# The entry of a windowed attention stage: three engines in written order, the first keys' norm moved behind the first queries' norm, and more projection columns ahead of the S5 tables

## The chip, the core and the metric

The kernel runs on one core of a Trainium2 chip. The metric is the device time of one execution in microseconds (us), the median of the runs. TensorE (PE in the profile, PEld its weight loads) does the matmuls, VectorE is DVE, ScalarE is ACT, GpSimd is POOL, and SP is the engine that issues most of the DMAs. PSUM is the memory that the matmuls write; a buffer of it is called a bank here.

## What is computed

One layer of a hybrid encoder over two sequences of 512 tokens with 1024 features, all in float32. Cut to what matters here:

```python
h = rms_norm(x, ln1)
q, k, v, u, g_att, g_ssm = split(h @ w_in)
q = rms_norm(q per head, q_gain); k = rms_norm(k per head, k_gain)   # 16 query heads, 4 key heads of 64
y_att = windowed_attention(q, k, v, sink, bias, mask)                # blocks of 128, each sees 3 key blocks
y_ssm = s5_branch(u, ...)     # bidirectional state-space scan in 64 groups, GELU, gated linear unit
mixed = sigmoid(g_att) * y_att + sigmoid(g_ssm) * y_ssm
x = x + mixed @ w_out
out = x + square(relu(rms_norm(x, ln2) @ w_up)) @ w_down
```

## The kernel before

Each float32 matmul is made of three, on a high part and a low part of both operands: high times high, high times low, low times high (`products`, L190, and `key_products`, L230). ScalarE writes the high part of a weight (`S.copy`, L180 for the columns, L1086 for whole blocks), VectorE subtracts it from the raw weight for the low part (L181, L1087).

**Fillers.** The projection of `u` and of the two gates is cut into 24 columns of 128 features; a column is computed for both sequences, 24 matmuls of 512 columns for each. Behind the 24 columns come the keys of the second sequence: four tiles of 128 tokens, 24 matmuls of 256 columns each (`key_products`), each tile followed by its norm: a square on ScalarE (L239), a sum on VectorE (L241), an add and a power of minus one half on GpSimd (L243, L244), and a multiply on VectorE (L247), which is the last to read the tile's bank. All of this is one generator, and `pull(n)` takes the next matmuls from it worth n units: a matmul of a column costs 2, one of a key tile 1. The other stages call `pull` between their own steps, so that TensorE has work while they wait. `phase["units"]` is what is left. While a column is computed, the weights of the next one are split into high and low parts at its fourth and tenth matmul, and the loads behind them are issued.

**Stages, in order.** First the norms and transposes of the input, with the coefficients of the state-space branch. Then the tables: `tables(c)` for c = 0 to 7, each in two steps q. A step makes `bpre` on VectorE (L592 to L595), transposes it on TensorE (L605) into `tps`, makes the table `ctab` on VectorE (L618 to L622), and pulls 44 units. The matmuls of the inputs with `u_sb` (L636) come one step later, and the lags (L548) every second step. Then the recurrence: 62 steps on VectorE (L711 to L714), with `pull(15)` after each. Then the outputs of the state-space branch: 32 steps of 12 matmuls (L745, L748), with a share of the remaining units after each, such that about 100 are left over; these are pulled after the last step. The tables `ctab`, the inputs `u_sb` and `toep` of that loop are loaded by GpSimd's queue two to three blocks of two steps ahead.

**The attention's entry** follows. The weights of the first query heads (`w_q`) and of the values (`w_v`) are loaded (`w_in`) and split in halves of 512 KB; the last key tile's multiply is done (`last_keys.pop()()`); for t = 0 to 3 a query tile of 128 tokens is projected (L915, 24 matmuls of 256 columns), squared on ScalarE (L921), summed (L925), raised to the power (L927, L928 on GpSimd) and multiplied (L932); the query tile before it is transposed (L937) and split (L942, L945); and a value tile of the second sequence is projected (`rows_block`, L121 to L123) and split (L849, L850). For t = 0 the keys `kn[:, 0:4]` of the first sequence, which were computed at the very start, are normed: a square into `k_sq` (L1110), a sum (L1111), add and power (L1112, L1113), and, behind the first value tile, the multiply (L1124) and the copy `kd` on GpSimd (L884). The transposes of these keys (`key_turn`, L897) come in the third round.

Every projection here takes its bank from one ring of three (`acc()`), in the order in which the program calls it; the second user after the next waits for the last reader of the first. In the entry the order is: the four key tiles, query tile 0, value tile 0, query tile 1, the transposes of query tile 0, value tile 1, query tile 2, and so on.

**Who sets the order.** Inside `tc.manual_schedule(engines={...})` the engines listed run their instructions in the order in which the program writes them. The other engines are ordered by a planner with its own estimate of costs: among the instructions that it holds for ready it takes the one that the program writes first. In the tables only TensorE and GpSimd are listed; in the output loop TensorE, ScalarE and VectorE; in the attention's entry only VectorE; in the attention itself all but SP.

## Time and profile before

| | |
|---|---|
| median of 3 runs | 1470.11 us (1470.04 to 1471.46) |
| the profiled execution, its own time | 1468.74 us |
| its span in the profile | 1467.0 us |
| TensorE busy | 1441.2 us, 98% of the span |
| VectorE, ScalarE, GpSimd busy | 1099.3, 764.4, 234.2 us |
| moved by DMA | 240.23 MB, 164 GB/s in the mean |

The profile's busy times add up the instructions of an engine; a bracket behind a row of the timeline gives the idle time of the engine ahead of it and what ended that. The views by windows give for each engine its busy us and the number of its instructions, then PEclk, the share of its full clock that TensorE was granted, the share of the DMA engines' time, and the rate in GB/s.

### The profile page before, as it was taken

The numbers are of one execution on the slowest core, as the hardware profiler recorded it, in microseconds if no ns is written. First come the engines' busy times: TensorE is split into PE (matmuls) and PEld (weight loads), VectorE is DVE, ScalarE is ACT, GpSimd is POOL, SyncE is SP. The second block draws the span as 40 slices with busy tenths as digits, with TensorE's granted clock in tenths as the row PEclk, the third lists the DMA queues.
The fourth block names the chain that finished last, engine by engine and source line by source line (L and its number), as shares of the span: only waits on it lengthen the run. The fifth ranks groups of instructions, "written<-read, shape, count | busy, mean of one in ns | idle before, by whom it ended". The sixth has DMA issues, their size and how long they took to land.

```text
span 1467.0 us, 22018 instructions
## 1 busy us (share of the span) xinstructions
PE 1441.2 (98%) x7981; PEld 1228.4 (84%) x7981; DVE 1099.3 (75%) x1985; ACT 764.4 (52%) x1361; POOL 234.2 (16%) x386
## 2 busy tenths in 40 slices
PE   8899999999989999999999999999999999999998
PEld 6688888889979999987888888888888888888887
DVE  7999949995436899988985578777776588575653
ACT  7588852224336888786443345544544444333332
POOL 3144452004233433252100000000000000000000
PEclk9999999999999999999999999999999999999999
DMA  7256649428750533345553245444443883454441
GB/s 292 94 156 184 191 132 337 158 101 292 260 178 20 175 95 108 97 160 167 185 193 113 88 140 198 148 154 144 146 149 115 326 324 125 158 177 153 129 129 58
DMA packets 102204, 240.23 MB, mean 164 GB/s; under 512 B 12330, under 2 KB 25130, under 8 KB 102096
## 3 DMA queue, kind: packets, MB, share of 16 engines
q1 hardware_dynamic: 62160, 139.68, 29.5%
q0 software_dynamic: 16320, 48.28, 9.9%
q10 hardware_dynamic: 23616, 50.87, 9.3%
q8 instruction: 63, 1.03, 0.3%
q14 instruction: 45, 0.37, 0.1%
HBM read 169.02 MB, written 81.82 MB: 171 GB/s over the span
## 4 chain that ended last, share of the span: by engine, by line
PE 85%; DVE 6%; DMA 3%; ACT 2%; issue 2%; POOL 1%; SPq 0%; DVEq 0%; ACTq 0%; POOLq 0%
PE acc L190 17%; PE bank L121 13%; PE bank L122 13%; PE bank L123 13%; PE acc L915 5%; PE acc L123 2%; PE acc L121 2%; PE acc L122 2%; PE acc L128 2%; PE sps L636 2%; PE po L998 2%; PE sps L748 2%; PE sps L966 2%; PE tps L982 2%; PE acc L343 1%
## 5 line engine op out<-in xcount | busy, mean ns | idle before, releaser
L190 PE MATMUL acc<-act,c_hi 128*128 128x512 f32 x768 | 244.4, 396 | 0.0
L122 PE MATMUL bank<-b_lo,a_hi 128*128 128x512 f32 (+1 forms) x449 | 174.6, 389 | 0.1
L121 PE MATMUL bank<-b_hi,a_hi 128*128 128x512 f32 (+1 forms) x449 | 174.5, 389 | 0.0
L123 PE MATMUL bank<-b_hi,a_lo 128*128 128x512 f32 (+1 forms) x449 | 174.5, 389 | 0.0
L190 PEld LDWEIGHTS acc<-act,c_hi 128*128 128x128 f32 x768 | 142.8, 189 | 28.2 <-ACT act L316 0.9
L1649 ACT CAST a_hi<-d_a 128x1024 fp32r<-128x1024 f32 x56 | 59.0, 1054 | 177.9 <-PE bank L122 174.6
L190 PE MATMUL acc<-act,c_lo 128*128 128x512 f32 x384 | 151.4, 394 | 0.0
L121 PE MATMUL bank<-act,act 128*128 128x512 f32 x368 | 143.2, 389 | 0.3 <-DVE tx L1437 0.3
L123 PE MATMUL bank<-act,act 128*128 128x512 f32 x368 | 143.2, 389 | 0.0
L122 PE MATMUL bank<-act,act 128*128 128x512 f32 x368 | 143.2, 389 | 0.0
L1650 DVE TENSOR_TENSOR a_lo<-d_a,a_hi 128x1024 fp32r<-128x1024 f32 x56 | 68.5, 1223 | 97.0 <-ACT a_hi L1649 97.0
L915 PE MATMUL acc<-w_hi,act 128*128 128x256 f32 x512 | 115.6, 294 | 3.8 <-DVE keys L247 3.8
L122 PEld LDWEIGHTS bank<-b_lo,a_hi 128*128 128x128 f32 x449 | 84.3, 188 | 18.1 <-DVE b_lo L1650 0.5
L121 PEld LDWEIGHTS bank<-b_hi,a_hi 128*128 128x128 f32 x449 | 84.3, 188 | 17.4
L123 PEld LDWEIGHTS bank<-b_hi,a_lo 128*128 128x128 f32 x449 | 84.3, 188 | 17.3
L915 PEld LDWEIGHTS acc<-w_hi,act 128*128 128x128 f32 x512 | 88.2, 192 | 7.7 <-ACT w_hi L1086 4.0
L190 PEld LDWEIGHTS acc<-act,c_lo 128*128 128x128 f32 x384 | 72.5, 189 | 14.3
L976 ACT ACTIVATE p<-p,nmx 128x257 f32<-128x257 f32 (+1 forms) x128 | 72.1, 563 | 19.7 <-DVE nmx L970 17.6
L121 PEld LDWEIGHTS bank<-act,act 128*128 128x128 f32 x368 | 69.1, 188 | 14.8 <-issue 0.7
L128 PE MATMUL acc<-act,gc_hi 128*128 128x512 f32 x256 | 81.1, 394 | 0.2 <-ACT gc_hi L781 0.2
L123 PEld LDWEIGHTS bank<-act,act 128*128 128x128 f32 x368 | 69.1, 188 | 14.5
L122 PEld LDWEIGHTS bank<-act,act 128*128 128x128 f32 x368 | 69.1, 188 | 14.3
(356 smaller groups left out, 3424.4 us busy)
## 6 DMA issues: line engine op xcount, KB each, us to landing
d_a<-a_scr SPq DMA_DIRECT2D x56, 512.0 KB, 3.6
raws<-in_w_up_dram SPq DMA_DIRECT2D x32, 512.0 KB, 4.0
a_scr<-t ACTq DMA_DIRECT2D x64, 256.0 KB, 2.8
k<-in_w_down_dram SPq DMA_DIRECT2D x32, 512.0 KB, 5.9
c_raw<-in_w_ug_dram SPq DMA_DIRECT2D x48, 256.0 KB, 3.9
ct_scr<-ctab POOLq DMA_DIRECT2D x16, 512.0 KB, 5.4
ctab_in<-ct_scr POOLq DMA_DIRECT2D x16, 512.0 KB, 6.4
a_scr<-a ACTq DMA_DIRECT2D x32, 256.0 KB, 2.0
```

What stands on the lines that cost most here:

```text
L121: PE.matmul(ps, a[0], b[0], start=first, stop=False)
L122: PE.matmul(ps, a[0], b[1], start=False, stop=False)
L123: PE.matmul(ps, a[1], b[0], start=False, stop=last)
L128: PE.matmul(ps, w[wi][:, k, :], rows[yi], start=k + p == 0, stop=k == KT - 1 and p == 2)
L190: PE.matmul(ps, w[wi][:, k, :], hT[s][hi][:, k, :], start=n == 0, stop=n == 3 * KT - 1)
L636: PE.matmul(ps[:, i * P:(i + 1) * P], bm[:, ri, g, :], u_sb[:, gp * SH + g, :], start=True, stop=True)
L748: PE.matmul(o, ctab[:, g0 % SI + g, ri, 0:T * CH], st[:, ri, g].rearrange("p s k -> p (s k)"), start=False, stop=ri == 1)
L915: PE.matmul(self.ps, hT[sq][act][:, k, col:col + P], w[:, k % 4, :], start=i == 0, stop=i == 3 * KT - 1)
L966: PE.matmul(ps[:, 0:self.nk], qs, kk[:, self.k0 * P:self.k1 * P], start=i == 0, stop=i == 1)
L976: S.activation(p, p, AF.Exp, bias=self.nmx[:, h:h + 1], scale=-1.0, accum_out=self.sums[:, h, self.qb:self.qb + 1])
L1649: S.copy(hi, src)
L1650: V.tensor_sub(lo, src, hi.bitcast(F32))
```

## The change

Four edits. More units are pulled ahead of the tables (116 for 72). The output loop leaves 108 units over in place of 100, and its tail is no longer pulled behind it: the attention's entry pulls all but the last key tile at its head, and the last key tile behind the split of `w_q`. In the entry TensorE and ScalarE, too, run in written order. The norm of the first sequence's keys moves: square, sum and power from ahead of the first query tile's norm to behind the first value tile, the multiply and the copy from the first round to the second; and `k_sq` is a tile of the pool `ap` (tag `ya`, which the raw weights of `w_q` use) in place of the pool `evp` (tag `ev`, which the last columns use until they are stored).

```diff
             pending = []
-            pull(72)
+            pull(116)
             for c in range(KT):
                 tables(c)
...
-                pull(-(-(phase["units"] - 100) // (GROUPS // SH - q)))
+                pull(-(-(phase["units"] - 108) // (GROUPS // SH - q)))
...
             store_y(*full)
-            pull(phase["units"])
             order.close()
...
-        with tc.manual_schedule(engines={ET.DVE}):
+        with tc.manual_schedule(engines={ET.PE, ET.DVE, ET.Activation}):
+            pull(phase["units"] - 3 * KT)
             SP.dma_start(kn[:, 0:4], kv_scr[:, :, 0])
             w_q = whole_block(w_qkv[Q_BLK], wq, "ya", 2)
             weights[0] = w_q
+            pull(phase["units"])
             w_v = whole_block(w_qkv[V_BLK], cpool, "p", 3)
             last_keys.pop()()
...
-            k_sq = evp.tile([P, NB, N_KV, HD], F32, tag="ev", name="k_sq")
...
                 new.project(3 * KT)
-                if t == 0:
-                    S.activation(k_sq, kn[:, 0:4], AF.Square, scale=HD ** -0.5)
-                    V.reduce_sum(ms, k_sq.rearrange("p t h d -> p (t h) d"), axis=AX.X)
-                    GP.tensor_scalar_add(ms, ms, EPS)
-                    GP.tensor_tensor(rk, ms, neg_half, op=ALU.pow)
                 new.square()
...
                 rows_block(w_v, NB + t, v_evac)
                 if t == 0:
+                    k_sq = ap.tile([P, NB, N_KV, HD], F32, tag="ya", name="k_sq")
+                    S.activation(k_sq, kn[:, 0:4], AF.Square, scale=HD ** -0.5)
+                    V.reduce_sum(ms, k_sq.rearrange("p t h d -> p (t h) d"), axis=AX.X)
+                    GP.tensor_scalar_add(ms, ms, EPS)
+                    GP.tensor_tensor(rk, ms, neg_half, op=ALU.pow)
+                if t == 1:
                     V.tensor_mul(kn[:, 0:4], kn[:, 0:4],
                                  rk.rearrange("p (t h) -> p t h", t=NB)[:, :, :, None].to_broadcast([P, NB, N_KV, HD]))
                     kd = key_copies(0, 0)
-                if t == 1:
                     S.copy(va[:, 0:4, :, 0:HD], vn)
```

## The prediction

> **What bounds the kernel now.** I read the page's head, then TensorE's waits, then the timeline of the engines around the longest of them, then windows for the granted clock, and the chain of waits between 400 and 455 us.

> ```profile
> span 1467.0 us, 22018 instructions
> PE 1441.2 (98%) x7981; PEld 1228.4 (84%) x7981; DVE 1099.3 (75%) x1985; ACT 764.4 (52%) x1361; POOL 234.2 (16%) x386
> ...
> PE tps L605 <- issue: 4.9, 1, 4.9
> PE acc L915 <- DVE keys L247: 3.8, 1, 3.8
> PE acc L937 <- DVE qn L932: 3.0, 2, 2.9
> ```

> TensorE is busy all but 26 us. Less work on another engine gives nothing; what counts is a hole in TensorE's row and the slow stretch behind it. Three long waits lie where the diff works: one ahead of the tables, two in the attention's entry. The hole ahead of the tables:

> ```profile
> 60.74 0.39 PE L190 MATMUL acc<-act,c_lo 128*128 128x512 f32 x1
> 66.00 2.10 PE L605 MATMUL tps<-ident,bpre 128*128 128x128 f32 x8 [4.88 <-issue]
> 73.98 1.95 PE L636 MATMUL sps<-u_sb,bm 128*128 128x128 f32 x16
> 75.77 1.04 PE L605 MATMUL tps<-ident,bpre 128*128 128x128 f32 x8
> ...
> 65.22 1.28 DVE L595 TENSOR_TENSOR bpre<-tb,bpre 128x512 f32<-128x512 f32 x2
> 70.44 0.69 DVE L181 TENSOR_TENSOR c_lo<-c_raw,c_hi 128x512 fp32r<-128x512 f32 x1
> 72.84 1.29 DVE L595 TENSOR_TENSOR bpre<-tb,bpre 128x512 f32<-128x512 f32 x2
> ...
> 66.25 0.62 ACT L180 CAST c_hi<-c_raw 128x512 fp32r<-128x512 f32 x1 [3.30 <-DMA c_raw<-in_w_ug_dram]
> ```

> The 72 units end at 61.12; the first transposes need `bpre`, which VectorE finishes only around 66. The profile calls the releaser "issue", but the engine that ends last is VectorE. The two holes in the entry:

> ```profile
> 409.33 0.38 ACT L239 ACTIVATE keys<-acc 128x256 f32<-128x256 f32 x1 [1.87 <-PE acc L230]
> 416.13 1.06 ACT L1110 ACTIVATE k_sq<-kn 128x1024 f32<-128x1024 f32 x1 [6.41 <-DMA gs_scr<-sg]
> 418.12 0.38 ACT L239 ACTIVATE keys<-acc 128x256 f32<-128x256 f32 x1
> 421.20 0.42 DVE L247 TENSOR_TENSOR keys<-acc,rk 128x256 f32<-128x256 f32 x1 [1.25 <-POOL rk L244]
> 417.65 0.28 PE L230 MATMUL acc<-c_hi,act 128*128 128x256 f32 x1
> 421.77 0.55 PE L915 MATMUL acc<-w_hi,act 128*128 128x256 f32 x1 [3.84 <-DVE keys L247]
> ...
> 428.45 1.21 DVE L1111 TENSOR_REDUCE k_ms<-k_sq 128x16 f32<-128x1024 f32 x1
> 429.27 0.37 ACT L849 CAST va<-acc 128x256 fp32r<-128x256 f32 x1 [2.49 <-PE acc L123]
> 430.10 2.93 POOL L1113 TENSOR_TENSOR k_rs<-k_ms,neg_half 128x16 f32<-128x16 f32 x1
> 433.43 1.04 POOL L928 TENSOR_TENSOR rq<-ms,neg_half 128x4 f32<-128x4 f32 x1
> 434.50 0.42 DVE L932 TENSOR_TENSOR qn<-acc,rq 128x256 f32<-128x256 f32 x1 [4.51 <-POOL rq L928]
> 434.98 0.73 PE L937 MATMUL acc<-ident,qn 128*64 128x128 f32 x4 [2.88 <-DVE qn L932]
> ```

> ScalarE squares the first key tile at 409.33, then stands 6.41 us in front of `k_sq`, whose buffer is still being stored to `gs_scr`. The second key tile is complete one tile later, near 412.2, but its square runs at 418.12, so its bank is multiplied and freed at 421.6. Query tile 0 uses that bank and waits 3.84 us. Then GpSimd's one queue: the power for the 16 first-key columns (2.93 us) stands ahead of that of query tile 0 (1.04 us), and the transposes of query tile 0 wait 2.88 us.

> Each hole is followed by a slow stretch:

> ```profile
> 63.00:63.50 0.50, 0.00 (x0) 0.00 (x0) 0.50 (x2) 0.00 (x0) 0.00 (x0) 0.81 0.00 0
> 66.00:70.00 4.00, 4.00 (x13) 3.25 (x14) 4.00 (x7) 3.66 (x14) 0.00 (x0) 0.50 0.19 68
> 421.80:425.30 3.50, 3.50 (x17) 3.50 (x18) 2.03 (x5) 1.29 (x2) 1.26 (x2) 0.53 0.28 104
> 435.00:439.00 4.00, 4.00 (x21) 3.96 (x22) 2.12 (x4) 0.68 (x1) 1.88 (x3) 0.57 0.00 0
> 260.00:325.00 65.00, 65.00 (x288) 53.81 (x288) 62.79 (x160) 15.89 (x27) 0.00 (x0) 1.00 0.33 117
> ```

> The sixth figure behind the times of a window is the granted clock. At half clock, half the stretch is lost: 4.0 x 0.50 = 2.0 us, 3.5 x 0.47 = 1.65 us, 4.0 x 0.43 = 1.7 us. The three places cost 4.88 + 2.0, 3.84 + 1.65 and 2.88 + 1.7: 17.0 us.

> **44 more units ahead of the tables.** 22 matmuls. In the undisturbed window 260 to 325 us 288 take 65.0 us, 0.226 each; so 22 take 4.97 us and end at 61.12 + 4.97 = 66.09, where the transposes start at 66.00 today. The hole is filled, minus 0.1. No work is added: the same matmuls are missing later, in the output loop, where TensorE is busy throughout, and that is where the time comes back. Price if the cover fails: the second half of column 3's weights is now written ahead of the tables, so the planner may put its low part (70.44 today) ahead of `bpre`; it needs its cast, 66.25 + 0.62, then 0.68, and the two subtractions behind it would start near 67.5 in place of 65.2. That costs up to 2.3 us. I take 0, because the planner let the tables pass today's waiting halves too; both ends stay in the range.

> The slow stretch goes with the hole (2.0 us), but VectorE, busy without a gap here, caps it: TensorE would reach the second transposes at 75.77 + 0.1 - 2.0 = 73.9, and the second `bpre` ends at 74.1. I take 1.7, ends 0 and 2.0. Recurrence and lags start behind TensorE's own work and move with it.

> **108 for 100, and the tail pulled in the entry.** Four matmuls, 0.9 us, run behind the loop instead of in it; TensorE's total is unchanged. With the 44 units the loop loses 52 units, 26 matmuls, 5.9 us, and its loads have that much less time. Cost zero while the loads stay ahead (rival below). `kn` and `w_in` gain 0.9 us before the key tiles.

> **`k_sq` in `ya`, behind value tile 0; written order on ScalarE.** Nothing on ScalarE then stands between the key tiles' squares, except the casts of `w_q`. Walked with the durations of the rows, on today's clock:

> ```profile
> 440.01 2.88 PE acc L915 x24
> ...
> L1086 ACT CAST w_hi<-w_in x8: 603/616/632, 417.1 to 421.5; 128x512 fp32r<-128x512 f32 x8
> L1087 DVE TENSOR_TENSOR w_lo<-w_in,w_hi x8: 681/686/693, 417.7 to 426.5; 128x512 fp32r<-128x512 f32 x8
> L1084 SPq DMA_DIRECT2D w_in<-in_w_qkv_dram x4: 469/489/750, 404.8 to 406.6; - x4
> ...
> DMA to landing us min/median/max: 6.7/10.1/11.3
> ```

> Key tiles come every 2.88 us: squares at 409.33, 412.2, 415.1, 418.0. The second's bank is free near 414.5, before query tile 0 wants it at 417.93: the 3.84 us go, and 1.65 with them. Behind the third square come the four casts of `w_q` (0.6 each, to 417.5; halves land from 411.5), VectorE's four low parts (0.69 each, to 418.7), the third key multiply (419.1, frees value tile 0's bank, wanted at 420.8), the casts of `w_v`, low parts to 422 and the last key multiply at 422.4 (frees query tile 1's bank, wanted at 423.7). No wait, with 1.3 us to spare at the tightest.

> TensorE's own order was this already: keys, query 0, value 0, query 1, turn 0, value 1. Listing it changes nothing.

> **The first keys' norm behind the first queries'.**

> ```profile
> 443.34 0.42 DVE L925 TENSOR_REDUCE ms<-sq 128x4 f32<-128x256 f32 x1 [1.33 <-ACT sq L921]
> 445.24 0.42 DVE L932 TENSOR_TENSOR qn<-acc,rq 128x256 f32<-128x256 f32 x1 [1.47 <-POOL rq L928]
> 442.89 0.44 PE acc L937 x4
> ```

> With GpSimd free, sum to multiply takes 1.9 us; query tile 0 is complete near 420.8, its multiply ends near 424.3, its transposes come after query tile 1 at 426.6: 2.88 + 1.7 go. What is late next: GpSimd is not listed, `k_ms` is written and ready ahead of query tile 1's sum, so the 2.93 us power now stands in front of that one. Counted from r, the start of value tile 0's copy (L849): `k_sq` r + 0.4 to r + 1.4; then today's stretch from the key sum (428.45) to the query multiply (434.50), 6.05; multiply 0.42; 0.15 to the matmul, as at 421.77: r + 8.1. Query tile 2 takes the bank of query tile 1. TensorE's way there: query 1, 2.88; turn, 0.44; value 1, 2.88: r + 6.2. A new wait of 1.9 us. Ends: 0 (GpSimd takes the query first) and 3.6, with a slow stretch of 1.7 behind it. Behind that multiply stand on VectorE the low part of turn 0, the key multiply and the value halves; key copies and key transposes are wanted some 6 us later.

> Does 1.9 us of idle lower the clock? At 63.0 to 63.5 the mean grant is 0.81, so it fell at 63.3, only 2.2 us after TensorE stopped; in the entry it fell after 2.88. Waits under 1 us show no fall. 1.9 is nearer to 2.2: I give the fall a chance of 0.35 and take none.
> [...]

> **Sum.** 4.88 - 0.1 + 1.7 + 3.84 + 1.65 + 2.88 + 1.7 - 1.9 = 14.65 us. The profiled execution took 1468.74 (span 1467.0 and 1.7 around it): 1454.1. It is 1.4 below the median of 1470.11, which gives 1455.5; part of that spread may be these holes' own, so I take 1455.0.

> **Rivals.**
> 1. The new wait also drops the clock: +1.7, 1456.7. For it: the fall at 2.2 us. [...]
> 2. The tables take it back: the low part of column 3 ahead of `bpre` (2.3) and VectorE capping the clock's gain (1.7): 1455 + 4 = 1459. For it: no gap on VectorE there. Against: column splits only move by one step of 44 units, so VectorE's total per table is the same.
> 3. The output loop becomes bound by its loads.

> ```profile
> 335.00:395.00 60.00, 60.00 (x413) 55.02 (x413) 31.93 (x43) 27.00 (x48) 24.01 (x34) 1.00 0.91 315
> ```

> The DMA engines are busy 0.91; a loop 5.9 us shorter than today's 77 needs 0.91 x 77 / 71 = 0.98 before counting the half column of weights that leaves it. If the loop keeps its length, the 5.9 us come back: 1460.9.

> 4. GpSimd takes query tile 1 first: no new wait, 1453.1.
> 5. Slower than before: the written order puts the last key tile's square behind the casts of `w_q`, and every bank behind it. Should `w_in` land late, all of it stops. Issued by 406.6 and landing after at most 11.3, the last is there at 417.9, its cast wanted near 419. It loses from there on, one for one; all 14.65 and 2.9 more are lost only if it lands near 437.

> **Chances.** Forecast (one wait, no slow stretch) 0.45; rival 1, 0.22; rival 2, 0.13; rival 3, 0.08; rival 4, 0.07; rival 5, with some loss 0.05, of it 0.02 beyond the start. 0.2%, 2.9 us, is about what a measurement here tells from no change: faster 0.95, same 0.03, slower 0.02. The range goes from rival 4 less the 1.4 of the profiled execution (1451.5) to rival 3's near end (1460.5).

> **What would show it.** TensorE's waits without `L605 <- issue` and without `L915 <- DVE keys`; the granted clock at 1.00 behind 66 us; the wait `L937 <- DVE qn` gone and one of about 1.9 us at L915 for DVE `qn`, with the 16-column power between two query powers on GpSimd; `k_sq` on ScalarE behind the first `va`; the output loop at 2.2 us a step for 2.4, with no wait at L745 or L748. The forecast is wrong if waits for `bpre` appear in the tables, if the loop waits for `toep` or `ctab_in`, or if ScalarE waits for `w_in`.

## The result, and the profile after

| | before | after |
|---|---|---|
| median of 4 runs each | 1470.78 us (1470.04 to 1472.18) | 1460.94 us (1458.60 to 1463.04) |
| ratio | | 0.9932, 95% interval 0.9914 to 0.9949 |
| profiled execution, and its span | 1468.74 us, 1467.0 us | 1461.13 us, 1459.3 us |

The change gains 9.8 us where 15.1 were forecast. The first two lines of the page after, then TensorE's waits (us in total, times, longest):

```profile
span 1459.3 us, 22019 instructions
...
PE 1439.5 (99%) x7981; PEld 1226.0 (84%) x7981; DVE 1098.9 (75%) x1985; ACT 764.3 (52%) x1361; POOL 236.2 (16%) x386
```

```profile
PE acc L343 <- ACT act L332: 6.4, 1, 6.4
PE bank L121 <- ACT act L1410: 2.1, 1, 2.1
PE acc L914 <- DVE qn L931: 1.7, 1, 1.7
PE acc L128 <- ACT gc_hi L780: 1.0, 1, 1.0
...
PE acc L128 <- DVE gc_lo L781: 0.7, 1, 0.7
```

(The lines of the attention stand one lower than before: L915 is L914, L932 is L931.) The three holes of before, 4.9 ahead of the tables, 3.8 and 2.9 in the entry, are gone. The new wait for `qn` was forecast. Nobody forecast the 2.1 at the first `bank`, which is the stage of the upward projections, nor the 1.0 and 0.7 at L128, which is the gated linear unit that closes the attention.

To see where the time went, the same instruction is looked up in both timelines, at the borders of the stages. First before, then after:

```profile
405.14 0.28 PE L230 MATMUL acc<-c_hi,act 128*128 128x256 f32 x1
660.93 0.39 PE L128 MATMUL acc<-act,gc_lo 128*128 128x512 f32 x1
769.39 0.39 PE L122 MATMUL acc<-act,act 128*128 128x512 f32 x1
890.62 0.39 PE L122 MATMUL bank<-t,act 128*128 128x512 f32 x1
```

```profile
67.68 1.39 PE L605 MATMUL tps<-ident,bpre 128*128 128x128 f32 x8
400.06 0.28 PE L230 MATMUL acc<-c_hi,act 128*128 128x256 f32 x1
649.24 0.39 PE L128 MATMUL acc<-act,gc_lo 128*128 128x512 f32 x1
759.48 0.39 PE L122 MATMUL acc<-act,act 128*128 128x512 f32 x1
882.94 0.39 PE L122 MATMUL bank<-t,act 128*128 128x512 f32 x1
```

| border | after minus before | of it in this stage | forecast |
|---|---|---|---|
| tables begin (66.00 before) | +1.68 | +1.68, at the start (see below) | 0 |
| second sequence's keys begin | -5.08 | -6.76 | -6.48 |
| last products of the attention | -11.69 | -6.61 | -8.17 |
| output projection | -9.91 | **+1.78** | 0 |
| upward projections | -7.68 | **+2.23** | 0 |

The sum is -7.68, and the spans differ by 7.7. The 1.68 arises at the start, since the 22 matmuls now pulled ahead of the tables only fill the hole that stood there. 1.0 of it is TensorE's first wait, L343: 5.4 us before, 6.4 after, and between 5.4 and 6.4 in all the profiles of this study, whatever the kernel. Most of the rest is TensorE's pace there: the first 128x512 matmuls start 0.46 us apart and later ones 0.23, and the slow pace ends at 8.7 us before and at 11.2 after, 3.3 and 4.8 us behind the first matmul. By an estimate from these rows that is 0.7 us. The views give the granted clock as 1.00 in that stretch, so its cause is not shown. Neither belongs to the change. The two bold terms are what the forecast did not have.

The three places in the timeline of after, with the idle time in brackets:

```profile
421.68 2.92 POOL L1123 TENSOR_TENSOR k_rs<-k_ms,neg_half 128x16 f32<-128x16 f32 x1
425.00 1.04 POOL L927 TENSOR_TENSOR rq<-ms,neg_half 128x4 f32<-128x4 f32 x1
426.55 0.39 PE L914 MATMUL acc<-w_hi,act 128*128 128x256 f32 x1 [1.74 <-DVE qn L931]
...
686.18 0.38 SPq L1047 DMA_DIRECT2D mix_scr<-ya  x1
690.03 1.14 DVE L807 TENSOR_TENSOR yy<-act,act 128x512 f32<-128x512 f32 x1 [1.35 <-DMA mix_scr<-ya]
716.64 0.73 PE L128 MATMUL acc<-act,gc_hi 128*128 128x512 f32 x2 [0.96 <-ACT gc_hi L780]
718.10 0.50 PE L128 MATMUL acc<-act,gc_lo 128*128 128x512 f32 x1 [0.73 <-DVE gc_lo L781]
...
855.28 0.68 DVE L1449 TENSOR_TENSOR f_sum<-acc,f_sum 128x512 f32<-128x512 f32 x1
856.11 0.47 PE L121 MATMUL bank<-act,act 128*128 128x512 f32 x1 [2.15 <-ACT act L1410]
```

The first group is the forecast wait: the 16-column power stands ahead of query tile 1's. In the second, VectorE waits for a store to be read out before it may write `yy`, and 27 us later TensorE pays for it (that the one follows from the other is shown below, by moving `k_sq` alone). In the third the releaser named (L1410) is not the one that counts: the first product starts when VectorE has added the last sum of the stage before (855.28 + 0.68 = 855.96). Before, there was no wait at either place:

```profile
697.53 0.38 SPq L1048 DMA_DIRECT2D mix_scr<-ya  x1
699.95 1.15 DVE L808 TENSOR_TENSOR yy<-act,act 128x512 f32<-128x512 f32 x1
863.32 0.39 PE L121 MATMUL bank<-act,act 128*128 128x512 f32 x1
```

Here `yy` is written 2.4 us behind the issue of the same store (3.8 after), and the first product follows the last sum's matmuls at once.

**The theory.** Two rings of buffers stand one place further. The addresses of the two built kernels say so. `ya` has two buffers, at 63616 and 67712 of each partition, and the later `yy` lies at 63456 to 65504, over the first. Before, the last `ya` lay in the second; after, `k_sq` takes a buffer of this ring, and the last `ya`, the one being stored, lies under `yy`. The three accumulator banks: the last three sums of the stage before the upward projections lay in banks 0, 2, 1 before and lie in 2, 1, 0 after, and the first product goes to bank 0 in both. The rivals: chance arrival of transfers, or an operand that is late whatever the bank.

### The profile page after: what moved, and what is told of

It is laid out like the page before. It is cut to its first block, busy times and chain, and to the rows that moved or that the text cites. A ratio compares the mean times of both kernels' runs of the same rounds, so it can differ in the third digit from the quotient of the medians.

```text
span 1459.3 us, 22019 instructions
## 1 busy us (share of the span) xinstructions
PE 1439.5 (99%) x7981; PEld 1226.0 (84%) x7981; DVE 1098.9 (75%) x1985; ACT 764.3 (52%) x1361; POOL 236.2 (16%) x386
## 4 chain that ended last, share of the span: by engine, by line
PE 87%; DVE 6%; ACT 3%; DMA 1%; issue 1%; POOL 1%; DVEq 0%; ACTq 0%; SPq 0%; POOLq 0%
PE acc L190 16%; PE bank L122 14%; PE bank L121 14%; PE bank L123 14%; PE acc L914 5%; PE acc L123 2%; PE acc L121 2%; PE acc L122 2%; PE acc L128 2%; PE sps L748 2%; PE po L997 2%; PE sps L636 2%; PE sps L965 2%; PE tps L981 2%; PE acc L343 1%
## 5 line engine op out<-in xcount | busy, mean ns | idle before, releaser
L190 PE MATMUL acc<-act,c_hi 128*128 128x512 f32 x768 | 244.1, 395 | 0.0
L123 PE MATMUL bank<-b_hi,a_lo 128*128 128x512 f32 (+1 forms) x449 | 174.5, 389 | 0.0
L190 PEld LDWEIGHTS acc<-act,c_hi 128*128 128x128 f32 x768 | 142.4, 188 | 28.1 <-ACT act L316 0.9
L190 PE MATMUL acc<-act,c_lo 128*128 128x512 f32 x384 | 151.2, 394 | 0.0
L123 PE MATMUL bank<-act,act 128*128 128x512 f32 x368 | 143.2, 389 | 0.0
L914 PE MATMUL acc<-w_hi,act 128*128 128x256 f32 x512 | 115.6, 294 | 1.7 <-DVE qn L931 1.7
L123 PEld LDWEIGHTS bank<-b_hi,a_lo 128*128 128x128 f32 x449 | 84.3, 188 | 17.1
L914 PEld LDWEIGHTS acc<-w_hi,act 128*128 128x128 f32 x512 | 88.2, 192 | 5.7 <-DVE qn L931 1.9
L190 PEld LDWEIGHTS acc<-act,c_lo 128*128 128x128 f32 x384 | 72.2, 188 | 14.0 <-DVE c_lo L181 0.2
L128 PE MATMUL acc<-act,gc_hi 128*128 128x512 f32 x256 | 81.2, 395 | 1.0 <-ACT gc_hi L780 1.0
L123 PEld LDWEIGHTS bank<-act,act 128*128 128x128 f32 x368 | 69.1, 188 | 14.5
```

The source lines that it names most:

```text
L123: PE.matmul(ps, a[1], b[0], start=False, stop=last)
L128: PE.matmul(ps, w[wi][:, k, :], rows[yi], start=k + p == 0, stop=k == KT - 1 and p == 2)
L190: PE.matmul(ps, w[wi][:, k, :], hT[s][hi][:, k, :], start=n == 0, stop=n == 3 * KT - 1)
L914: PE.matmul(self.ps, hT[sq][act][:, k, col:col + P], w[:, k % 4, :], start=i == 0, stop=i == 3 * KT - 1)
```

## The experiments

### Either half of the change alone, and the first ring

The control is the changed kernel as it is.

> The changed kernel unaltered, as the control of this group. Theory (rotated buffers): the change's 13.3 us up to the attention's entry are paid back in part because two rings of buffers stand one place further: ya, which costs 1.8 us at the start of the stage that closes the attention (VectorE's yy waits for a store to mix_scr), and the accumulator banks, which cost 2.2 us at the first product of the upward projections. Both come from addresses, so both waits stand here again, at the same two places, and the time is 9 to 11 us below the kernel before. Rival (chance arrival of transfers): these two waits are missing or have another size here, and the time moves by some 2 to 4 us against the first profile of the same kernel.

Measured: 1461.19 us (5 runs), ratio 0.9939 [0.9926, 0.9953]. The waits at the two places are there again (2.1 at the first `bank`, 1.1 and 0.6 at L128).

The pull counts alone:

```diff
             pending = []
-            pull(72)
+            pull(116)
...
-                pull(-(-(phase["units"] - 100) // (GROUPS // SH - q)))
+                pull(-(-(phase["units"] - 108) // (GROUPS // SH - q)))
```

> The kernel before with nothing of the change but the counts 116 for 72 and 108 for 100; the entry is as before. The accumulator ring is rotated here as in the changed kernel, ya is not. Theory (rotated buffers): 6.7 us gained up to the keys, both holes of the entry as before (3.8 and 2.9 us), no wait of yy at the start of the closing stage, but the 2.2 us wait at the first product of the upward projections: about 4.5 us below the kernel before. Rival (the entry's edit costs both later waits): neither is here, 6.7 us below. Rival (chance): neither place repeats.

Measured: 1465.88 us (11 runs) beside 1470.43 before, ratio 0.9970 [0.9961, 0.9979], so 4.5 us gained as the theory has it. That it fits so well is in part luck: in its profile the entry is 1.2 us shorter than before, and a slow stretch behind the new wait takes 1.7 us. TensorE's waits:

```profile
PE acc L343 <- ACT act L332: 6.1, 1, 6.1
PE acc L915 <- DVE keys L247: 3.3, 1, 3.3
PE acc L937 <- DVE qn L932: 2.2, 1, 2.2
PE bank L121 <- ACT act L1410: 2.1, 1, 2.1
```

The entry's holes are still there, a little shorter, and the wait at the first `bank` has come with nothing but two numbers changed more than 450 us ahead of it. `yy` does not wait.

The edits of the entry alone: the after kernel with 72 and 100.

> The changed kernel with 72 and 100 put back, so only the edits of the entry. ya is rotated as in the changed kernel, the accumulator ring stands as in the kernel before. Theory (rotated buffers): the hole ahead of the tables stays (4.9 us), the entry gains 6.6 us, yy waits for the store to mix_scr (1.8 us), and there is no wait at the first product of the upward projections: about 4.8 us below the kernel before. Rival (the pull counts cost both later waits): no wait of yy, 6.6 us below. Rival (the entry's edit costs both): both waits, 2.6 us below.

Measured: 1465.18 us (6 runs), ratio 0.9968 [0.9957, 0.9980]: 5.3 us gained, 4.8 expected. The other way round: `yy` waits, the first `bank` does not. A row of VectorE, then TensorE's waits:

```profile
693.81 1.14 DVE L807 TENSOR_TENSOR yy<-act,act 128x512 f32<-128x512 f32 x1 [0.88 <-DMA mix_scr<-ya]
```

```profile
PE tps L605 <- issue: 4.8, 1, 4.8
PE acc L914 <- DVE qn L931: 1.7, 1, 1.7
...
PE bank L121 <- DVE tx L1437: 0.3, 1, 0.3
```

So the two costs have two causes, one in each half of the change. In the changed kernel, `k_sq` alone is now moved to another ring:

```diff
-                    k_sq = ap.tile([P, NB, N_KV, HD], F32, tag="ya", name="k_sq")
+                    k_sq = evp.tile([P, NB, N_KV, HD], F32, tag="ev", name="k_sq")
```

> The changed kernel with k_sq at its new place but in the buffer ev that it had before, so that ya's ring stands as in the kernel before. Theory (rotated buffers): the wait of yy for the store to mix_scr goes and the time is 1.8 us below the control's; the 2.2 us wait at the first product of the upward projections stays. The square does not wait for a store here, since the one to gs_scr landed at 416 us and k_sq is written behind 418 us. Rival (the wait of yy is a matter of the store's landing time, not of the buffer): the wait stays and the time equals the control's. Rival (ev's ring, now one place further, brings another wait of its own): 0 to 2 us above the theory.

Measured: 1458.18 us (5 runs), ratio 0.9917 [0.9904, 0.9931], 3.0 us below the control where 1.8 were expected; the two intervals overlap a little. In the control's profile this stage also holds a slow stretch of the clock (1.7 us lost), here it holds none. The same store, the same `yy`, no wait, and the wait for `gc_hi` gone with it:

```profile
687.96 1.15 DVE L807 TENSOR_TENSOR yy<-act,act 128x512 f32<-128x512 f32 x1
```

Half a microsecond at `gc_lo` remains, as in the kernel with the entry's edits only (0.6). The first `bank` still waits 2.1.

### The second ring, a first try that moved the wait

```diff
-    for _ in range(6):
-        bank()
+    V.memset(bank()[0:1, 0:2], 0.0)
```

The six calls that go are of banks that no instruction uses; they are not in the built kernel, with or without this edit.

> The changed kernel with one edit ahead of the upward projections: a first bank that VectorE writes two elements of is put ahead of the first product, so that the product goes to the next bank (7) and no longer to the one whose last sum VectorE is still adding. Theory (rotated buffers): the 2.15 us wait of the first product goes, and with it the slow stretch of 1.7 us that three of the four profiles with this wait show behind it; 2.2 to 3.9 us below the changed kernel (about 1457 to 1459), the two waits at gc_hi and gc_lo of 1.7 us together stay. Rival (the first product waits for its operand, a square root of the order and not the bank): the wait stays, time as the changed kernel. Rival (the next products take the wait over): a wait of some 2 us one or two products later.

Measured: 1461.17 us (5 runs), ratio 0.9945 [0.9933, 0.9958]: no gain. The timeline says why:

```profile
851.10 0.39 PE L121 MATMUL bank<-act,act 128*128 128x512 f32 x1
856.98 0.47 PE L121 MATMUL bank<-act,act 128*128 128x512 f32 x1 [2.99 <-DVE bank L1535]
...
856.15 0.68 DVE L1437 TENSOR_TENSOR tx<-tx,tps 128x512 f32<-128x512 f32 x1
```

The first product now follows at once. The second has moved on as well, from bank 7 to bank 6, which held a `tps` that VectorE reads until 856.83; it waits 2.99. The write that I added follows that read on VectorE and is the releaser that the profile names; the matmul starts 0.15 us behind the end of the read, as the first product of the changed kernel did behind the last sum (855.96 to 856.11). The third rival came true: the wait was handed on.

> The changed kernel with both rings put where they do no harm: k_sq in ev, the first product of the upward projections in bank 7. The entry's order is the changed kernel's. This is the change as the prediction reckoned it, with nothing paid back behind the entry. Theory (the prediction's sum up to the attention is right, and only the rings failed it): 1455 us without the slow stretch behind the new wait, 1456.7 with it, some 5 us below the changed kernel. Rival (part of the sum ahead of the attention was too high as well): 1458 or more, without a wait behind the attention's entry that is not in the kernel before.

Measured: 1460.45 us (5 runs), ratio 0.9932 [0.9919, 0.9944], with the same 3.0 us at the second product: 4 to 5 us above the theory, and no verdict on the sum.

### Query tile 1 ahead of the first keys

```diff
                 new.square()
                 new.power()
+                if t == 1:
+                    V.reduce_sum(ms, k_sq.rearrange("p t h d -> p (t h) d"), axis=AX.X)
+                    GP.tensor_scalar_add(ms, ms, EPS)
+                    GP.tensor_tensor(rk, ms, neg_half, op=ALU.pow)
                 new.norm()
```

(and the same three lines taken out behind value tile 0)

> The changed kernel with the sum, the addition and the power of k_sq moved behind query tile 1's sum of squares (the square itself stays behind value tile 0), so that GpSimd raises query tile 1 first. Theory: the 1.74 us wait of query tile 2 for qn goes and so does the slow stretch of 1.7 us that three of four profiles show behind it: 1.7 to 3.4 us below the changed kernel (about 1457.5 to 1459.5). GpSimd ends the 16 columns near 427, VectorE's multiply and the key copies end near 430, and the key transposes are wanted near 431: no wait there. Rival (the wait only moves): the key transposes or query tile 3's bank wait 1 to 2 us for kd or qn, time as the changed kernel.

Measured: 1458.49 us (5 runs), ratio 0.9923 [0.9910, 0.9937]. GpSimd's order is turned round, and the 1.74 us are gone but for half a microsecond at query tile 3:

```profile
422.00 1.03 POOL L927 TENSOR_TENSOR rq<-ms,neg_half 128x4 f32<-128x4 f32 x1
423.46 2.93 POOL L1114 TENSOR_TENSOR k_rs<-k_ms,neg_half 128x16 f32<-128x16 f32 x1
...
431.20 0.39 PE L914 MATMUL acc<-w_hi,act 128*128 128x256 f32 x1 [0.52 <-DVE qn L931]
```

> Both rings put right as in r2_both_rings, and query tile 1 ahead of the first keys on GpSimd as in r2_query_first. Theory: the three costs lie in different stages and add up: 1.7 to 3.4 us below r2_both_rings, about 1453 us, and 17 to 18 us below the kernel before; no fall of the clock between 60 and 1400 us. Rival (something else is late next in the entry): time as r2_both_rings, with a new wait at the key transposes or query tile 3.

Measured: 1457.12 us (4 runs), ratio 0.9917 [0.9904, 0.9931], 4 us above the theory; the second product waits 3.0 us here, too.

### The second ring put right

The banks follow from the order in which the pools are made. Another order puts the bank of `po`, long free, under the first product, and the third-last sum's under the second. No instruction changes.

```diff
-    ps_acc = front.enter_context(tc.tile_pool(name="ps_acc", bufs=3, space=PSUM))
+    ps_o = front.enter_context(tc.tile_pool(name="ps_o", bufs=1, space=PSUM))
     ps_s = front.enter_context(tc.tile_pool(name="ps_s", bufs=2, space=PSUM))
     ps_t = front.enter_context(tc.tile_pool(name="ps_t", bufs=2, space=PSUM))
-    ps_o = front.enter_context(tc.tile_pool(name="ps_o", bufs=1, space=PSUM))
+    ps_acc = front.enter_context(tc.tile_pool(name="ps_acc", bufs=3, space=PSUM))
```

> The kernel before with the accumulator pools created in that other order, as the control of the edit. Its last three sums lie in banks 5, 7 and 6, the first product's bank is po's, the second's is that of the second-last sum. Theory (an order of pools costs or gains only where a product meets a bank that is still read): no such wait here or in the kernel before, so the times agree within 0.1%. Rival (the order of the pools is worth something by itself): 2 us or more off the kernel before, and r3_pool_order's gain is not the ring's.

Measured on the kernel before: 1469.64 us (11 runs), ratio 0.9996 [0.9987, 1.0005]. The order alone makes no difference clear of the noise. Its profile has one small gain: from the first product to the border of the upward projections it takes 26.7 us for 27.3, and the 0.3 us wait that the kernel before has at its second product is gone.

> The changed kernel with the accumulator pools created in another order (ps_o, ps_s, ps_t, ps_acc), so that bank 0, which the first product of the upward projections takes, is the long-read one of po, bank 7 of the second product is the third-last sum, 6 and 5 come later. Nothing in the order of work differs. Theory (rotated buffers): no wait of 2.15 us at the first product and none of 2.99 us at the second (the first edit only moved the first product onto bank 7 and the second onto bank 6, which VectorE still reads in L1437); 2.2 to 3.9 us below the changed kernel, about 1457 to 1459. Rival (the upward stage is bound by VectorE's and ScalarE's operands, whatever the bank): the wait turns up again one or two products later with 2 to 3 us, time as the changed kernel.

Measured on the changed kernel: 1458.00 us (4 runs), ratio 0.9917 [0.9904, 0.9931]. No wait at any `bank` above 0.3 us; those of the entry and of `ya`'s ring stay:

```profile
PE acc L914 <- DVE qn L931: 1.7, 1, 1.7
PE acc L128 <- ACT gc_hi L780: 1.5, 1, 1.5
```

Both rings put right, the entry as in the change:

> The other order of the accumulator pools and k_sq in ev: both rings harmless, the entry as in the changed kernel. This is the change as the prediction reckoned it. Theory: 1455 us without the slow stretch behind the new wait of 1.74 us, 1456.7 with it; the waits behind the entry as in the kernel before. Rival (the sum ahead of the attention was too high too): 1458 or more without such a wait.

Measured: **1454.76 us** (1453.62 to 1455.44, 4 runs), ratio 0.9893 [0.9878, 0.9909]. The forecast was 1455.0.

And with query tile 1 first:

> As r3_both_rings, and the first keys' sum behind query tile 1's on VectorE, so that GpSimd raises query tile 1 first. Theory (the three costs add): 1.2 to 2.9 us below r3_both_rings, since 0.5 of the 1.74 us came back at query tile 3 in the run with that edit alone: 1453 to 1454 us, about 17 us below the kernel before, and no slow stretch between 60 and 1400 us. Rival: time as r3_both_rings.

Measured: **1453.17 us** (1452.24 to 1454.68, 4 runs) beside 1470.52 before, ratio 0.9886 [0.9873, 0.9900]. The interval lies wholly below that of the changed kernel (0.9914 to 0.9949): it beats both. Against the run before it the intervals overlap, so the 1.6 us of this last step are not clear of the noise. TensorE's waits:

```profile
PE acc L343 <- ACT act L332: 5.7, 1, 5.7
PE sps L965 <- DVE nmx L969: 0.9, 2, 0.5
...
PE acc L914 <- DVE qn L931: 0.5, 1, 0.5
```

No single wait above 0.7 us is left behind the start, and in no window of 1 us of this profile is the granted clock below 1.00.

## Why the prediction was wrong

**What held.** The fill of the hole ahead of the tables and the clock behind it: 6.48 forecast, 6.76 measured. The windows of after (TensorE's busy us and instructions, then the granted clock):

```profile
63.00:63.50 0.50, 0.50 (x4) 1.00 1.02 410
66.00:70.00 4.00, 3.86 (x22) 1.00 0.52 156
```

The output loop shows no wait at L745 or L748 after, so rival 3 fell (but it stands close: other builds with the same counts wait 0.2 to 0.9 us there for `ctab_in`); VectorE didn't take the tables back, so rival 2 fell. GpSimd took the first keys first (rival 4 fell), and TensorE waited for none of the weights of the entry (rival 5 fell). In the entry both holes went, and the new wait came at the place, from the cause and with the size that were forecast: 1.74 us for 1.9.

**What was judged the wrong way.** Whether that wait drops the clock: a chance of 0.35, and none was taken. In this profile it does, as rival 1 had it:

```profile
424.19:427.60 3.41, 1.68 (x14) 1.00 0.00 0
427.60:431.01 3.41, 3.41 (x18) 0.50 0.00 0
```

3.41 us at 0.50 lose 1.7 us, and the entry gained 6.61 for 8.17. In the three profiles that have this wait and no slow stretch behind it the entry gains 8.08 to 8.15, so the other terms of its sum came out right together. The argument for no fall compared 1.9 us with the 2.2 that had passed from TensorE's stop at 61.12 to the fall at 63.31; what the other falls say to that is told under the hardware below.

**The step that failed** is the sum itself: it ends with the entry and takes what is gained there for gained at the end. Of the move it says "`k_sq` in `ya`" and prices the store that `k_sq` no longer waits for; it doesn't ask what every later user of the ring `ya` does with its buffer. Of the pulls it says that "no work is added", which is true; it doesn't ask which bank each later sum gets when the sums are handed out in another order. Each missed a term: +1.78 us, shown by the run that moves only `k_sq`, and +2.23, shown by the run that moves only the banks, in several profiles with 1.7 us of slow clock behind it. Between the same instructions as in the table of borders, the closing stage takes 108.46 us before, 110.24 after and 108.40 with `k_sq` in `ev`; the stretch from there to the upward projections takes 121.23, 123.46 and, with the other order of the pools, 120.97. In the profiles the sum is short by 6.97 us (14.65 forecast, 7.68 gained): 1.78 and 2.23 are the two rings, 1.56 the slow clock in the entry, 1.68 the start, less 0.28 gained more at the tables.

With both rings put right, the forecast time comes out (1454.76 for 1455.0). That it comes out to a quarter of a microsecond is luck: that profile has no slow stretch behind the entry's wait, and the order of the pools also takes away the half microsecond that the kernel before lost behind its first product. The range failed for the same reason as the sum: none of the five rivals had a cost behind the entry, so its upper end was rival 3's. Both ends are also off their own working: rival 4 less 1.4 is 1451.7, not 1451.5, and rival 3 was worked out as 1460.9, not 1460.5.

So the border of two pools is a place to check: there the first product met a bank whose last sum was still being read and waited 2.15 us, and with a long free bank in its place (the other order of the pools, `r3_pool_order`) no wait at any `bank` was above 0.3 us.

That the ring's place follows from the counts of a pull is shown by the runs; how the planner came to hand out the banks in that order was not followed further.

## What to carry to other kernels

An edit that takes one more buffer from a ring, or hands out the same buffers in another order, moves every later user of that ring. Compare the addresses of the two builds at the borders of the stages, where the next pool lies over the ring: the last buffer written or stored ahead of a border should not be the first one that the next stage takes. When a gain at one place comes out smaller at the end, subtract the two timelines border by border: the stage that pays it back is seen at once.

## What the hardware showed

Between the start and the last 10 us of the span, every slow stretch in the profiles here has a granted clock of 0.50 and lasts 3.40 to 3.42 us, 1.7 us lost, but for three of 6.82 us, 3.4 us lost: at 63.31 behind the hole of 4.9 us in the kernel before; at 63.28 behind one of 4.8 with the entry's edits alone (`r1_entry_only`); and at 421.24 behind one of 3.7 in the kernel before with the other order of the pools (`r3_before_pools`). Whether a wait is followed by one can't be told from the wait's length alone. Of the eight kernels here with the 1.72 to 1.74 us wait in the entry, five showed the slow stretch behind it in their profile and three did not. Of the five profiles with the 2.15 us wait, four showed the stretch, and the one of the changed kernel above did not. All three with the 2.99 us wait did. In the control it also came at 716 us, behind two waits of 1.09 and 0.56 us close to each other.

Nor does the fall come at a fixed time behind TensorE's stop. Before, TensorE stops at 61.12, 417.93 and 432.10 and the clock falls at 63.31, 421.71 and 435.36, which is 2.19, 3.78 and 3.26 us later; after, it stops at 424.81 and the clock falls 2.79 us later, when TensorE has been at work again for 1.05. So the 2.2 us of the prediction were not a delay that a wait has to reach.

```profile
423.92:427.33 3.41, 2.10 (x17) 1.00 0.00 0
427.33:430.75 3.42, 3.42 (x31) 1.00 0.00 0
...
424.35:427.76 3.41, 1.73 (x14) 1.00 0.00 0
427.76:431.17 3.41, 3.41 (x31) 1.00 0.00 0
```

For a sum this means a term with a chance. A wait of 1.74 us lies whole in one step of 3.41 us in about half of all cases (an estimate from these two figures: 1.67 of 3.41), and five of eight were seen; so 1.7 us times a half or somewhat more. It is part of the spread between runs of one kernel, which is 2 to 6 us here: the fastest run of the control took 1457.81 us at a mean granted clock of 1.000, the profiled one, with three slow stretches, 1461.75 at 0.996.
